# LayerNorm with a residual on one core: rows in DRAM blocks of 24, 24 and 16 per partition, and another list of 27 transfers

## The chip, the core and the metric

The kernel runs on one core of one Trainium2 chip. Its time is the device time of one execution in microseconds (us); the time of a version is the median over several runs. Before the change it is 237.93 us, from three runs between 237.87 and 237.95.

## What is computed

Two float32 tensors of 16 x 1024 x 512 are added, and each of the 16,384 rows of 512 numbers is normalised (mean, variance), scaled and shifted:

```python
def reference(x, residual, gamma, beta, eps):
    z = x + residual
    mean = np.mean(z, axis=-1, keepdims=True)
    var = np.var(z, axis=-1, keepdims=True)
    z_norm = (z - mean) / np.sqrt(var + eps)
    return (gamma * z_norm + beta).astype(np.float32)
```

x and residual are 33.55 MB each and so is the output: 100.66 MB have to be moved between DRAM and the core's memory (SBUF).

## The kernel before

The 16,384 rows are dealt to 128 partitions, so that each partition has 128 rows, and all counts below are rows per partition: one such row over all partitions is 128 x 512 numbers of 4 bytes, 262,144 bytes. The function `dram` (L73) says which rows of the DRAM tensor belong to which partition: the tensor is cut into blocks of `BLOCK` = 64 rows per partition, and within a block partition p has 64 rows that lie one behind the other in DRAM. A transfer must stay within one block (L65). A transfer of n rows takes from each partition one unbroken piece of n x 2 KiB; the pieces of two neighbouring partitions start 64 x 2 KiB = 128 KiB apart.

Two buffers in SBUF hold the data as rings: `zbuf` with 64 rows (x first, and later the results, in the same place), `rbuf` with 32 rows (residual first, then the sum). Row lo stands in slot lo modulo 64, or modulo 32.

`PLAN` (L19) is a list of words such as `x32+16`, load 16 rows of x from row 32 on; `r` is the residual, `o` a store of finished rows. SyncE (SP) issues the transfers strictly in this order at L140, all on one queue, and waits ahead of an issue where it has to:

- a load of x into slots that were used already waits until the stores of those rows have landed (L148, semaphores `so`),
- a load of residual into used slots waits until VectorE has read them (L154, `s_rstd` of the turn that read the last of them),
- a store waits until VectorE has finished its rows (L158, `s_out`).

While SP waits, all later issues of the list wait too. The first two issues (`EARLY`) are moved ahead of the barrier at the start of the program (L277).

The computation goes in turns of four rows, 32 turns:

- GpSimd (POOL) waits until the loads of both tensors that hold these rows have landed, and adds four rows in one instruction, rbuf = zbuf + rbuf (L178).
- ScalarE (ACT) waits for the sum and takes four row means with an accumulating activation (L201, a running sum of -z/512), four sums of squares (L211) and one square root for the four rows (L220). The activations' full results go to scratch (`junk_m`, `junk_s`).
- VectorE (DVE) waits for the square root, writes (sum - mean) x gamma into zbuf for four rows (L239), then the reciprocal of the root (L247), which also says that these rows of rbuf are free, and then multiplies by it and adds beta (L253), which says that the rows may be stored.

TensorE only spreads gamma and beta over the partitions at the start. ACT and DVE run loops, of 32 rows and of 64 rows per lap.

Of the kernel before, what the change touches and what calls it, by code (L numbers as in the profile page):

```python
# [8 lines left out]
FP32 = mybir.dt.float32  # L9
# [1 line left out]
ALU = mybir.AluOpType  # L11


BLOCK = 64
Z_ROWS = 64
R_ROWS = 32


PLAN = """  # L19
x0+8 r0+8 x8+8 r8+8 x16+16 r16+16 x32+16 r32+16 x48+16  # L20
o0+16 r48+16 x64+12 o16+20 r64+16 x76+24 r80+16 o36+28
r96+16 x100+8 x108+20 r112+4 r116+12
o64+16 o80+28 o108+12 o120+4 o124+4
"""


ADDS = [4] * 32


TURN = 4  # L30
R_TURNS = R_ROWS // TURN
Z_TURNS = Z_ROWS // TURN


EARLY = 2
# [3 lines left out]
def kernel(  # L39
# [9 lines left out]
    nc = tc.nc  # L49
    P = nc.NUM_PARTITIONS  # L50
# [3 lines left out]
    N, D = xf.shape  # L54
    inv_d = 1.0 / float(D)
    total = N // P


    tc.close()
    tc.compile()  # L60
# [1 line left out]
    moves = []  # L62
    for word in PLAN.split():
        kind, (lo, n) = word[0], map(int, word[1:].split("+"))
        assert lo // BLOCK == (lo + n - 1) // BLOCK  # L65
        moves.append((kind, lo, n))

    def of_kind(kind):
# [3 lines left out]

    def dram(t, lo, n):  # L73

        b0 = lo - lo % BLOCK
        v = t[P * b0 : P * (b0 + BLOCK), :].rearrange("(p j) d -> p j d", p=P)
        return v[:, lo - b0 : lo - b0 + n, :].rearrange("p a b -> p (a b)")

    zbuf = nc.alloc_sbuf_tensor("zbuf", [P, Z_ROWS * D], FP32)
# [4 lines left out]
    nm, ssq, std, rstd = (  # L84
        nc.alloc_sbuf_tensor(name, [P, R_ROWS], FP32) for name in ("nm", "ssq", "std", "rstd")
    )
    gamma_p = nc.alloc_psum_tensor("gamma_p", [P, D], FP32)
    beta_p = nc.alloc_psum_tensor("beta_p", [P, D], FP32)
    junk_m = [nc.alloc_psum_tensor(f"junk_m{i}", [P, D], FP32) for i in range(TURN)]
    junk_s = [nc.alloc_psum_tensor(f"junk_s{i}", [P, D], FP32) for i in range(6 - TURN)]  # L90
    junk_s += [
        nc.alloc_sbuf_tensor(f"junk_s{i}", [P, D], FP32) for i in range(6 - TURN, TURN)
    ]

    sems = []
# [1 line left out]
    def sem(name):  # L97
        s = nc.alloc_semaphore(name)
        sems.append(s)
        return s  # L100
# [5 lines left out]
    s_const = sem("const")  # L106
    s_pe = sem("pe")
    s_sum, s_mean, s_ssq, s_std = (
        [sem(f"{name}{j}") for j in range(R_TURNS)] for name in ("sum", "mean", "ssq", "std")
    )  # L110
    s_rstd = [sem(f"rstd{j}") for j in range(Z_TURNS)]
    s_out = sem("out")
    so = [sem(f"so{c}") for c in range(len(stores))]
    nums = [s.num for s in sems]
# [2 lines left out]
    def part(buf, size, lo, n):  # L117
        assert lo % size + n <= size
        return buf[:, (lo % size) * D : (lo % size + n) * D]
# [16 lines left out]
    seen = 0  # L136
    first = []

    def move(out, in_, s):
        i = nc.sync.dma_start(out=out, in_=in_).then_inc(s, 16)  # L140
        if len(first) < EARLY:
            first.append(i.ins)

    gone = 0
    for kind, lo, n in moves:
        if kind == "x":
            while gone < len(stores) and stores[gone][0] < lo + n - Z_ROWS:
                nc.sync.wait_ge(so[gone], 16)  # L148
                gone += 1
            move(part(zbuf, Z_ROWS, lo, n), dram(xf, lo, n), sx[loads_x.index((lo, n))])  # L150
        elif kind == "r":
            if lo + n > R_ROWS:
                last = (lo + n - R_ROWS) // TURN - 1
                nc.sync.wait_ge(s_rstd[last % Z_TURNS], last // Z_TURNS + 1)  # L154
            move(part(rbuf, R_ROWS, lo, n), dram(rf, lo, n), sr[loads_r.index((lo, n))])
        else:
            if lo + n > seen:
                nc.sync.wait_ge(s_out, lo + n)  # L158
                seen = lo + n
            move(dram(of, lo, n), part(zbuf, Z_ROWS, lo, n), so[stores.index((lo, n))])  # L160


# [5 lines left out]


    landed = {"x": 0, "r": 0}  # L170
    lo = 0
    for n in ADDS:
        for key, loads, s in (("x", loads_x, sx), ("r", loads_r, sr)):
            while landed[key] < len(loads) and loads[landed[key]][0] < lo + n:
                nc.gpsimd.wait_ge(s[landed[key]], 16)  # L175
                landed[key] += 1
        z = part(rbuf, R_ROWS, lo, n)
        nc.gpsimd.tensor_tensor(  # L178
            out=z, in0=part(zbuf, Z_ROWS, lo, n), in1=z, op=ALU.add
        ).then_inc(s_sum[lo // TURN % R_TURNS], 1)  # L180
        lo += n
    assert lo == total

# [1 line left out]
    def column(t, lo, n=1):  # L187
        return t[:, lo % R_ROWS : lo % R_ROWS + n]
# [5 lines left out]
    with act.Fori(0, total // R_ROWS) as lap:  # L194
        hints.append(act.mark_branch_hint_location())  # L195
        due = act.snap(lap + 1)
        for j in range(R_TURNS):
            rows = range(j * TURN, (j + 1) * TURN)
            act.wait_ge(s_sum[j], due)  # L199
            for k, r in enumerate(rows):  # L200
                i = act.activation(  # L201
                    out=junk_m[k][:, :],
                    in_=part(rbuf, R_ROWS, r, 1),
                    func=ACT.Identity,
                    scale=-inv_d,
                    accum_out=column(nm, r),
                )
            i.then_inc(s_mean[j], 1)
            act.wait_ge(s_mean[j], due)
            for k, r in enumerate(rows):  # L210
                i = act.activation(  # L211
                    out=junk_s[k][:, :],
                    in_=part(rbuf, R_ROWS, r, 1),
                    func=ACT.Square,
                    bias=column(nm, r),
                    accum_out=column(ssq, r),
                )
            i.then_inc(s_ssq[j], 1)
            act.wait_ge(s_ssq[j], due)
            act.activation(  # L220
                out=column(std, rows[0], TURN),
                in_=column(ssq, rows[0], TURN),
                func=ACT.Sqrt,
                bias=eps_t[:, 0:1],
                scale=inv_d,
            ).then_inc(s_std[j], 1)


    dve = nc.vector
    dve.wait_ge(s_pe, 2)  # L230
    with dve.Fori(0, total // Z_ROWS) as lap:  # L231
        hints.append(dve.mark_branch_hint_location())
        due = [dve.snap(lap * 2 + 1), dve.snap(lap * 2 + 2)]
        turn = dve.snap(lap + 1)
        for j in range(Z_TURNS):
            rows = range(j * TURN, (j + 1) * TURN)
            dve.wait_ge(s_std[j % R_TURNS], due[j // R_TURNS])
            for r in rows:
                dve.scalar_tensor_tensor(  # L239
                    out=part(zbuf, Z_ROWS, r, 1),  # L240
                    in0=part(rbuf, R_ROWS, r, 1),
                    scalar=column(nm, r),
                    in1=gamma_p[:, :],
                    op0=ALU.add,
                    op1=ALU.mult,
                )
            dve.reciprocal(  # L247
                out=column(rstd, rows[0], TURN), in_=column(std, rows[0], TURN)
            ).then_inc(s_rstd[j], 1)
            dve.wait_ge(s_rstd[j], turn)  # L250
            for r in rows:
                z = part(zbuf, Z_ROWS, r, 1)
                i = dve.scalar_tensor_tensor(  # L253
                    out=z,
                    in0=z,
                    scalar=column(rstd, r),
                    in1=beta_p[:, :],
                    op0=ALU.mult,
                    op1=ALU.add,
                )  # L260
            i.then_inc(s_out, TURN)


    loops = [b for b in nc.main_func.blocks if b.name.endswith("_loop")]
# [48 lines left out]
```

## Time and profile before

| | |
|---|---|
| median of the runs | 237.93 us |
| profiled execution, its own time | 237.87 us |
| its span, first to last instruction | 236.5 us |
| moved over DMA | 100.68 MB, mean 426 GB/s |
| ACT busy | 183.8 us, 78% |
| DVE busy | 177.2 us, 75% |
| POOL busy | 144.1 us, 61% |
| POOL waits for residual loads | 62.1 us, 9 times |
| ACT waits for POOL | 32.5 us, 6 times |
| SP waits for DVE's reciprocal (free slots of rbuf) | 126.9 us, 6 times |
| SP waits for finished rows (stores) | 54.8 us, 6 times |
| SP waits for landed stores (free slots of zbuf) | 33.6 us, 3 times |

How to read it: busy times are those of the engine's own instructions, within the span. SP's own waits are not busy time and cost nothing by themselves: the queue goes on with what SP issued earlier. The profiled execution has its own time; the 1.4 us between that and the span lie around the first and the last instruction.

The groups of instructions of one turn, with the count, the total busy time and the mean of one in ns, and behind the bar the idle time of the engine ahead of them:

```profile
L178 POOL TENSOR_TENSOR rbuf<-zbuf,rbuf 128x2048 f32<-128x2048 f32 x32 | 143.9, 4526 | 66.6 <-DMA rbuf<-in_residual_dram 62.1
L239 DVE SCALAR_TENSOR_TENSOR zbuf<-rbuf,nm,gamma_p 128x512 f32<-128x512 f32 x128 | 87.1, 743 | 46.5 <-ACT std L220 46.5
L201 ACT ACTIVATE junk_m<-rbuf 128x512 f32<-128x512 f32 x128 | 74.3, 580 | 32.7 <-POOL rbuf L178 32.5
L211 ACT ACTIVATE junk_s<-rbuf,nm 128x512 f32<-128x512 f32 x128 | 88.8, 694 | 1.0
```

And a part of the chain of waits (start in us, length in us, what), one turn from POOL to DVE and the next load that DVE releases:

```profile
119.84 4.53 POOL rbuf L178
...
141.73 2.46 ACT junk_m L201 x8
144.19 0.02 issue
144.21 2.94 ACT junk_s L211 x8
147.15 0.03 issue
147.17 0.30 ACT std L220
147.48 0.02 issue
147.50 2.72 DVE zbuf L239 x4
150.22 0.10 DVE rstd L247
150.32 0.02 issue
150.34 20.26 DMA rbuf<-in_residual_dram
```

POOL's adds begin at 12.23 us (the first two turns) and, for the third load of residual, at 41.44 us.

### The profile page before, as it was taken

The numbers are of one execution on the slowest core, as the hardware profiler recorded it, in microseconds if no ns is written. First come the engines' busy times: TensorE is split into PE (matmuls) and PEld (weight loads), VectorE is DVE, ScalarE is ACT, GpSimd is POOL, SyncE is SP. The second block draws the span as 40 slices with busy tenths as digits, with TensorE's granted clock in tenths as the row PEclk, the third lists the DMA queues.
The fourth block names the chain that finished last, engine by engine and source line by source line (L and its number), as shares of the span: only waits on it lengthen the run. The fifth ranks groups of instructions, "written<-read, shape, count | busy, mean of one in ns | idle before, by whom it ended". The sixth has DMA issues, their size and how long they took to land.

```text
span 236.5 us, 992 instructions
## 1 busy us (share of the span) xinstructions
PE 3.7 (2%) x4; PEld 1.2 (0%) x4; DVE 177.2 (75%) x290; ACT 183.8 (78%) x545; POOL 144.1 (61%) x36
## 2 busy tenths in 40 slices
PE   0600000000000000000000000000000000000000
PEld 0100000000000000000000000000000000000000
DVE  0001999629999999589990999889993999999930
ACT  2019997299999996899909999899939999999400
POOL 0098920999799306993079846993199498960000
DMA  8999999999999999998999999989999999998997
GB/s 316 438 435 435 421 438 443 443 443 443 427 371 438 443 421 423 470 436 384 443 449 474 391 427 499 398 389 432 416 454 429 417 442 435 489 436 388 411 410 327
DMA packets 3893, 100.68 MB, mean 426 GB/s; under 512 B 434, under 2 KB 434, under 8 KB 436
## 3 DMA queue, kind: packets, MB, share of 16 engines
q1 hardware_dynamic: 3888, 100.67, 99.4%
q14 instruction: 1, 0.01, 0.0%
q10 hardware_dynamic: 4, 0.00, 0.0%
HBM read 67.11 MB, written 33.55 MB: 426 GB/s over the span
## 4 chain that ended last, share of the span: by engine, by line
ACT 48%; DMA 35%; POOL 6%; DVE 4%; issue 1%; SPq 1%; ACTq 0%; DVEq 0%; POOLq 0%
DMA rbuf<-in_residual_dram 35%; ACT junk_s L211 25%; ACT junk_m L201 21%; POOL rbuf L178 6%; DVE zbuf L239 3%; ACT std L220 2%; DVE zbuf L253 1%; SPq L140 1%; DVE rstd L247 0%; ACTq L194 0%; DVEq L231 0%; ACTq L199 0%; POOLq L175 0%; ACTq L195 0%
## 5 line engine op out<-in xcount | busy, mean ns | idle before, releaser
L178 POOL TENSOR_TENSOR rbuf<-zbuf,rbuf 128x2048 f32<-128x2048 f32 x32 | 143.9, 4526 | 66.6 <-DMA rbuf<-in_residual_dram 62.1
L239 DVE SCALAR_TENSOR_TENSOR zbuf<-rbuf,nm,gamma_p 128x512 f32<-128x512 f32 x128 | 87.1, 743 | 46.5 <-ACT std L220 46.5
L201 ACT ACTIVATE junk_m<-rbuf 128x512 f32<-128x512 f32 x128 | 74.3, 580 | 32.7 <-POOL rbuf L178 32.5
L211 ACT ACTIVATE junk_s<-rbuf,nm 128x512 f32<-128x512 f32 x128 | 88.8, 694 | 1.0
L253 DVE SCALAR_TENSOR_TENSOR zbuf<-zbuf,rstd,beta_p 128x512 f32<-128x512 f32 x128 | 87.1, 743 | 1.1
L201 ACT ACTIVATION_READ_ACCUMULATOR junk_m<-rbuf 128x1 f32 x128 | 23.9, 187 | 0.0
L211 ACT ACTIVATION_READ_ACCUMULATOR junk_s<-rbuf,nm 128x1 f32 x128 | 23.9, 187 | 0.0
L220 ACT ACTIVATE std<-ssq,eps_t 128x4 f32<-128x4 f32 x32 | 9.5, 297 | 1.0
L247 DVE RECIPROCAL rstd<-std 128x4 f32<-128x4 f32 x32 | 5.4, 170 | 0.0
L192 ACT ACT_TABLE_LOAD x1 | 1.3, 1283 | 2.7 <-PEq L60 2.7
L131 PE MATMUL gamma_p<-gb_row,ones 1*128 1x512 f32 x2 | 2.0, 1118 | 7.0 <-DMA gb_row<-in_gamma_dram 7.0
L131 PE MATMUL beta_p<-gb_row,ones 1*128 1x512 f32 x2 | 1.9, 1052 | 0.0
L126 DVE MEMSET ones<- 1x128 f32 x1 | 0.2, 165 | 2.0 <-PEq L60 2.0
L131 PEld LDWEIGHTS beta_p<-gb_row,ones 1*128 1x128 f32 x2 | 0.7, 327 | 1.0 <-issue 0.5
L131 PEld LDWEIGHTS gamma_p<-gb_row,ones 1*128 1x128 f32 x2 | 0.5, 308 | 7.0 <-issue 7.0
L294 POOL MEMSET const-float32-0.0<- 128x1 f32 x1 | 0.1, 100 | 0.2 <-issue 0.2
L294 POOL MEMSET const-bfloat16-1.0<- 128x1 bf16 x1 | 0.1, 103 | 0.0
L294 POOL MEMSET const-uint8-127<- 128x1 uint8 x1 | 0.1, 103 | 0.0
L294 POOL MEMSET const-float32-1.0<- 128x1 f32 x1 | 0.1, 100 | 0.0
L127 DVE MEMSET eps_t<- 128x1 f32 x1 | 0.1, 59 | 0.0
## 6 DMA issues: line engine op xcount, KB each, us to landing
rbuf<-in_residual_dram SPq DMA_DIRECT2D x6, 4096.0 KB, 21.5
out_dram<-zbuf SPq DMA_DIRECT2D x2, 7168.0 KB, 31.5
zbuf<-in_x_dram SPq DMA_DIRECT2D x3, 4096.0 KB, 28.8
out_dram<-zbuf SPq DMA_DIRECT2D x2, 4096.0 KB, 33.9
zbuf<-in_x_dram SPq DMA_DIRECT2D x3, 2048.0 KB, 14.5
zbuf<-in_x_dram SPq DMA_DIRECT2D x1, 6144.0 KB, 24.0
out_dram<-zbuf SPq DMA_DIRECT2D x1, 5120.0 KB, 28.9
zbuf<-in_x_dram SPq DMA_DIRECT2D x1, 5120.0 KB, 26.3
```

The lines of the kernel that those rows point to most:

```text
L126: nc.vector.memset(ones[:, :], 1.0).then_inc(s_const, 1)
L131: nc.tensor.matmul(dest[:, :], ones[:, :], gb_row[:, k * D : (k + 1) * D], start=True, stop=True).then_inc(s_pe, 1)
L140: i = nc.sync.dma_start(out=out, in_=in_).then_inc(s, 16)
L178: nc.gpsimd.tensor_tensor(out=z, in0=part(zbuf, Z_ROWS, lo, n), in1=z, op=ALU.add).then_inc(s_sum[lo // TURN % R_TURNS], 1)
L192: act.preload_act_table_set("sqrt_and_others")
L201: i = act.activation(out=junk_m[k][:, :], in_=part(rbuf, R_ROWS, r, 1), func=ACT.Identity, scale=-inv_d, accum_out=column(nm, r),)
L211: i = act.activation(out=junk_s[k][:, :], in_=part(rbuf, R_ROWS, r, 1), func=ACT.Square, bias=column(nm, r), accum_out=column(ssq, r),)
L220: act.activation(out=column(std, rows[0], TURN), in_=column(ssq, rows[0], TURN), func=ACT.Sqrt, bias=eps_t[:, 0:1], scale=inv_d,).then_inc ...
L239: dve.scalar_tensor_tensor(out=part(zbuf, Z_ROWS, r, 1), in0=part(rbuf, R_ROWS, r, 1), scalar=column(nm, r), in1=gamma_p[:, :], op0=ALU.ad ...
L247: dve.reciprocal(out=column(rstd, rows[0], TURN), in_=column(std, rows[0], TURN)).then_inc(s_rstd[j], 1)
L253: i = dve.scalar_tensor_tensor(out=z, in0=z, scalar=column(rstd, r), in1=beta_p[:, :], op0=ALU.mult, op1=ALU.add,)
L294: nc = _bacc.Bacc("TRN2", target_bir_lowering=False, num_devices=1)
```

## The change

The rows are dealt to the partitions in blocks of 24, 24 and 16 rows, repeated (0 to 23, 24 to 47, 48 to 63, 64 to 87, 88 to 111, 112 to 127), in place of blocks of 64. The pieces of neighbouring partitions then start 48 KiB apart in blocks of 24 and 32 KiB apart in blocks of 16. A transfer of a whole block reads or writes one unbroken region of DRAM.

The list of transfers is another one; it has 27 words as before (6 of x, 12 of residual, 9 stores, where it had 9, 10 and 8). Every load of x is a whole block. The first load has 24 rows; the residual comes in loads of 8 and 16 rows. The rest of the diff makes the sizes of blocks and turns lists with a look-up (`edges`, `spot`), and with `TURNS = [4]` every turn has four rows, as before. The instructions of TensorE, VectorE, ScalarE and GpSimd are the same in number, form and order.

```diff
-BLOCK = 64
+BLOCKS = [24, 24, 16]

 PLAN = """
-x0+8 r0+8 x8+8 r8+8 x16+16 r16+16 x32+16 r32+16 x48+16
-o0+16 r48+16 x64+12 o16+20 r64+16 x76+24 r80+16 o36+28
-r96+16 x100+8 x108+20 r112+4 r116+12
-o64+16 o80+28 o108+12 o120+4 o124+4
+x0+24 r0+8 r8+16 x24+24 r24+8 x48+16 r32+16 o0+16 o16+8
+r48+16 x64+24 r64+16 o24+24 r80+8 r88+8 x88+24 r96+8 o48+16
+r104+8 r112+8 x112+16 r120+8 o64+24 o88+24 o112+8 o120+4 o124+4
 """
-ADDS = [4] * 32
-TURN = 4
+TURNS = [4]
...
+    def edges(sizes, end):
+        found, k = [0], 0
+        while found[-1] < end:
+            found.append(found[-1] + sizes[k % len(sizes)])
+            k += 1
+        assert found[-1] == end
+        return found
+
+    def spot(marks, row):
+        return max(k for k, m in enumerate(marks) if m <= row)
+
+    blocks = edges(BLOCKS, total)
+    marks = edges(TURNS, total)
...
     def dram(t, lo, n):
-        b0 = lo - lo % BLOCK
-        v = t[P * b0 : P * (b0 + BLOCK), :].rearrange("(p j) d -> p j d", p=P)
+        k = spot(blocks, lo)
+        b0, b1 = blocks[k], blocks[k + 1]
+        v = t[P * b0 : P * b1, :].rearrange("(p j) d -> p j d", p=P)
         return v[:, lo - b0 : lo - b0 + n, :].rearrange("p a b -> p (a b)")
...
             if lo + n > R_ROWS:
-                last = (lo + n - R_ROWS) // TURN - 1
-                nc.sync.wait_ge(s_rstd[last % Z_TURNS], last // Z_TURNS + 1)
+                last = spot(marks, lo + n - R_ROWS - 1)
+                nc.sync.wait_ge(s_rstd[last % z_turns], last // z_turns + 1)
...
             if lo + n > seen:
-                nc.sync.wait_ge(s_out, lo + n)
-                seen = lo + n
+                seen = next(m for m in marks if m >= lo + n)
+                nc.sync.wait_ge(s_out, seen)
```

More of the change, by code (lines that the diff above doesn't have):

```diff
@@ L19 @@
 PLAN = """
-x0+8 r0+8 x8+8 r8+8 x16+16 r16+16 x32+16 r32+16 x48+16
-o0+16 r48+16 x64+12 o16+20 r64+16 x76+24 r80+16 o36+28
-r96+16 x100+8 x108+20 r112+4 r116+12
-o64+16 o80+28 o108+12 o120+4 o124+4
-"""
-ADDS = [4] * 32
-TURN = 4
-R_TURNS = R_ROWS // TURN
-Z_TURNS = Z_ROWS // TURN
+x0+24 r0+8 r8+16 x24+24 r24+8 x48+16 r32+16 o0+16 o16+8
+r48+16 x64+24 r64+16 o24+24 r80+8 r88+8 x88+24 r96+8 o48+16
+r104+8 r112+8 x112+16 r120+8 o64+24 o88+24 o112+8 o120+4 o124+4
+"""
+TURNS = [4]
 EARLY = 2
@@ L56 @@
     total = N // P
+    def edges(sizes, end):
[9 more added lines that the diff above has]
+    marks = edges(TURNS, total)
+    most = max(TURNS)
+    r_turns, z_turns = spot(marks, R_ROWS), spot(marks, Z_ROWS)
+    assert marks[r_turns] == R_ROWS and marks[z_turns] == Z_ROWS
+    assert z_turns == 2 * r_turns
     tc.close()
@@ L64 @@
         kind, (lo, n) = word[0], map(int, word[1:].split("+"))
-        assert lo // BLOCK == (lo + n - 1) // BLOCK
+        assert spot(blocks, lo) == spot(blocks, lo + n - 1)
         moves.append((kind, lo, n))
@@ L88 @@
     beta_p = nc.alloc_psum_tensor("beta_p", [P, D], FP32)
-    junk_m = [nc.alloc_psum_tensor(f"junk_m{i}", [P, D], FP32) for i in range(TURN)]
-    junk_s = [nc.alloc_psum_tensor(f"junk_s{i}", [P, D], FP32) for i in range(6 - TURN)]
+    junk_m = [nc.alloc_psum_tensor(f"junk_m{i}", [P, D], FP32) for i in range(most)]
+    junk_s = [nc.alloc_psum_tensor(f"junk_s{i}", [P, D], FP32) for i in range(6 - most)]
     junk_s += [
-        nc.alloc_sbuf_tensor(f"junk_s{i}", [P, D], FP32) for i in range(6 - TURN, TURN)
+        nc.alloc_sbuf_tensor(f"junk_s{i}", [P, D], FP32) for i in range(6 - most, most)
     ]
@@ L108 @@
     s_sum, s_mean, s_ssq, s_std = (
-        [sem(f"{name}{j}") for j in range(R_TURNS)] for name in ("sum", "mean", "ssq", "std")
+        [sem(f"{name}{j}") for j in range(r_turns)] for name in ("sum", "mean", "ssq", "std")
     )
-    s_rstd = [sem(f"rstd{j}") for j in range(Z_TURNS)]
+    s_rstd = [sem(f"rstd{j}") for j in range(z_turns)]
     s_out = sem("out")
@@ L170 @@
     landed = {"x": 0, "r": 0}
-    lo = 0
-    for n in ADDS:
+    for k in range(len(marks) - 1):
+        lo, n = marks[k], marks[k + 1] - marks[k]
         for key, loads, s in (("x", loads_x, sx), ("r", loads_r, sr)):
@@ L179 @@
             out=z, in0=part(zbuf, Z_ROWS, lo, n), in1=z, op=ALU.add
-        ).then_inc(s_sum[lo // TURN % R_TURNS], 1)
-        lo += n
-    assert lo == total
+        ).then_inc(s_sum[k % r_turns], 1)
     def column(t, lo, n=1):
@@ L196 @@
         due = act.snap(lap + 1)
-        for j in range(R_TURNS):
-            rows = range(j * TURN, (j + 1) * TURN)
+        for j in range(r_turns):
+            rows = range(marks[j], marks[j + 1])
             act.wait_ge(s_sum[j], due)
@@ L220 @@
             act.activation(
-                out=column(std, rows[0], TURN),
-                in_=column(ssq, rows[0], TURN),
+                out=column(std, rows[0], len(rows)),
+                in_=column(ssq, rows[0], len(rows)),
                 func=ACT.Sqrt,
@@ L234 @@
         turn = dve.snap(lap + 1)
-        for j in range(Z_TURNS):
-            rows = range(j * TURN, (j + 1) * TURN)
-            dve.wait_ge(s_std[j % R_TURNS], due[j // R_TURNS])
+        for j in range(z_turns):
+            rows = range(marks[j], marks[j + 1])
+            dve.wait_ge(s_std[j % r_turns], due[j // r_turns])
             for r in rows:
@@ L247 @@
             dve.reciprocal(
-                out=column(rstd, rows[0], TURN), in_=column(std, rows[0], TURN)
+                out=column(rstd, rows[0], len(rows)), in_=column(std, rows[0], len(rows))
             ).then_inc(s_rstd[j], 1)
@@ L260 @@
                 )
-            i.then_inc(s_out, TURN)
+            i.then_inc(s_out, len(rows))
     loops = [b for b in nc.main_func.blocks if b.name.endswith("_loop")]
```

## The prediction

> **What bounds the kernel now.** I read the page's DMA rows first, then the stretches, then the SP issues in order of time, then the chain of waits. DMA rows of the page:
>
> ```profile
> DMA  8999999999999999998999999989999999998997
> DMA packets 3893, 100.68 MB, mean 426 GB/s; under 512 B 434, under 2 KB 434, under 8 KB 436
> q1 hardware_dynamic: 3888, 100.67, 99.4%
> ```
>
> The one queue that SP feeds is busy 99.4% of the span. 3888 is 27 transfers x 144: 128 data packets (one per partition) and 16 small ones each. The next view cuts the span into stretches; the last two columns are the DMA engines' busy share and GB/s.
>
> ```profile
> 0.00:6.00 6.00, 0.00 (x0) 0.00 (x0) 0.17 (x2) 1.28 (x1) 0.20 (x4) 1.00 0.86 320
> 6.00:18.00 12.00, 3.74 (x4) 1.15 (x4) 0.00 (x0) 1.25 (x5) 5.77 (x2) 1.00 1.01 430
> 18.00:60.00 42.00, 0.00 (x0) 0.00 (x0) 30.05 (x49) 35.46 (x107) 30.14 (x7) 1.00 1.01 434
> 60.00:80.00 20.00, 0.00 (x0) 0.00 (x0) 19.02 (x33) 19.58 (x59) 18.00 (x4) 1.00 1.01 423
> 80.00:120.00 40.00, 0.00 (x0) 0.00 (x0) 35.52 (x59) 35.02 (x105) 18.14 (x5) 1.00 1.01 434
> 120.00:160.00 40.00, 0.00 (x0) 0.00 (x0) 31.57 (x52) 34.11 (x102) 33.81 (x8) 1.00 1.00 433
> 160.00:200.00 40.00, 0.00 (x0) 0.00 (x0) 34.90 (x58) 36.06 (x109) 27.07 (x7) 1.00 1.00 429
> 200.00:230.00 30.00, 0.00 (x0) 0.00 (x0) 26.00 (x43) 21.02 (x64) 10.98 (x3) 1.00 1.00 433
> 230.00:236.50 6.50, 0.00 (x0) 0.00 (x0) 0.00 (x0) 0.00 (x0) 0.00 (x0) 1.00 0.77 324
> ```
>
> No long stretch exceeds 434 GB/s, whether it only loads (18 to 60) or mostly stores (200 to 230: 433). At 434 the 100.68 MB take 232.0 us; the span is 236.5, so 4.5 are lost, and each stretch's share is its length x (1 - GB/s / 434): start 1.58, 6 to 18 0.11, 60 to 80 0.51 (the first store falls there), 120 to 160 0.09, 160 to 200 0.46, 200 to 230 0.07, end 1.65. Sum 4.47. Start and end belong to any plan; 1.24 us in the middle is all that a plan could win.
>
> SP waits long, yet nothing starves, because it issues ahead:
>
> ```profile
> 42.70 0.33 SPq L140 DMA_DIRECT2D rbuf<-in_residual_dram  x1
> 71.94 0.33 SPq L140 DMA_DIRECT2D rbuf<-in_residual_dram  x1
> 80.99 0.33 SPq L140 DMA_DIRECT2D zbuf<-in_x_dram  x1
> 110.23 0.33 SPq L140 DMA_DIRECT2D zbuf<-in_x_dram  x1
> 226.90 0.33 SPq L140 DMA_DIRECT2D out_dram<-zbuf  x1
> ```
>
> I call "lead" the time from an issue until the queue has drained what stands ahead. One row of all partitions is 262,144 B, 0.604 us at 434 GB/s, so the transfers ahead have drained at 1.6 + 0.604 x their rows. For these five (r32+16, r48+16, x64+12, x76+24, o124+4: 80, 128, 144, 192, 380 rows ahead) that is 49.9, 78.9, 88.6, 117.6, 231.1, and the leads are 7.2, 7.0, 7.6, 7.4 and 4.2 us. So the chain of waits, which names ACT for 48%, doesn't set the end: it only has to keep the leads above nothing.
>
> **The change part by part.**
>
> *Transfers.* Still 27 (x 9 to 6, r 10 to 12, o 8 to 9), the same bytes, one packet per partition, hence again 3888 packets: 0 us. The 27 issues of 0.33 to 0.48 us lie inside leads. The first two issues still stand ahead of the start barrier and the last store is still 4 rows: start 1.58 and end 1.65 stay.
>
> *First load of 24 rows.* The first add needs x0+24 and r0+8, 32 rows where it was 16. Drained at 1.6 + 32 x 0.604 = 20.9; in before the same sum for 64 rows gives 40.3 and POOL started at 41.44, so 1.1 of landing: 22.0 against 12.23, 9.8 us later. What hides this is ACT's slack: it waits 32.5 us on POOL in before. Uncovered it would cost what exceeds the leads, so I follow the chain. POOL adds four rows in 4.5; ACT takes 5.75 per turn (2.46 + 2.94 + 0.30 and issue); DVE frees rbuf 2.85 after (2.72 + 0.10) and the rows are done 5.6 after. A load that waits for a store came 2.1 after the drain in before (o0+16: 78.9, x64+12 at 80.99).
>
> - r32+16 (waits for turn 3): 22.0 + 4.5 + 4 x 5.75 + 2.85 = 52.4; 96 rows ahead drain at 59.6; lead 7.2.
> - r48+16 (turn 7): 26.5 + 8 x 5.75 + 2.85 = 75.4; 136 rows, 83.7; lead 8.3.
> - x64+24 (waits for o16+8): 83.7 + 2.1 = 85.8; 152 rows, 93.4; lead 7.6.
> - r64+16 (turn 11; its first add needs r32+16, 112 rows): 69.2 + 1.1 + 4.5 + 4 x 5.75 + 2.85 = 100.7; 176 rows, 107.9; lead 7.2.
> - x88+24 (waits for o24+24, 216 rows): 132.1 + 2.1 = 134.2; 232 rows, 141.7; lead 7.5.
> - x112+16 (waits for o48+16, 280 rows): 170.7 + 2.1 = 172.8; 296 rows, 180.4; lead 7.6.
> - o88+24 (turn 27; turn 22 needs x88+24, 256 rows): 156.2 + 1.1 + 4.5 + 6 x 5.75 + 5.6 = 201.9; 344 rows, 209.4; lead 7.5.
> - o124+4: four turns later, 224.9; 380 rows, 231.1; lead 6.2.
>
> All others have more. The small residual loads in the second half add two waits on DVE (7 to 9); behind each stand the next issues of SP, x88, o48, r104 and so on, and all still come 7 us or more early. So every lead is as long as those with which before kept the queue at 1.00: 0 us. The nearest thing behind is turn 28: x112+16 lands at 191.1, its add ends at 195.6, ACT is free at 196.3; half a microsecond of slip there comes off leads of 6, not off the end.
>
> *Blocks.* Rows of one partition lie 48, 48 and 32 KiB apart per block instead of 128 KiB, and x loads of a whole block read one unbroken stretch of DRAM. No row of before shows another pitch, so I bound it. Best: everything lost in the middle goes, -1.24. Worst: the 33.55 MB of stores run at 423 instead of 434, the lowest long stretch: 79.3 - 77.3 = +2.0. I take 0, the nearest row being 434 for loads and 433 for stores, on either side the same figure, as if the queue's engines and not DRAM limited them.
>
> The Trainium skill ("DMA: Bandwidth & Descriptors", section on latency and other measured facts) reports that per-partition pitches of large powers of two cut a copy's rate (207 GB/s per direction at 512 KiB, 164 at 2 MiB, 103 at 4 MiB) and that a padded pitch restores it; it has no figure for 128 KiB, and 434 GB/s here leaves nothing to restore. By that rule the change could only win, by the rows nothing. "Perfetto Trace Analysis", section on DMA optimizations, speaks against the first part: smaller first pieces let work start sooner, where DMA engines are idle. By the rule the sum would be up to 237.87 + 9.8 = 247.7 with no lead; here the share is 1.01 from 6 us on, and the sum stays.
>
> *Sum.* 237.87 (profiled execution: span 236.5 and 1.4 around it; the median of the runs is 237.93) + 0 + 0 + 0 = 237.9.
>
> **The rivals.** (a) *The middle loss goes.* Block-wide loads avoid the 423 and 429 stretches: 0.51 + 0.46 and at most 1.24, so 236.6 to 237.4. For: 0.51 sits at one place, around the first store, and not at the later ones. Against: a first store comes in the new plan too, and five of the seven stretches between start and end are at 430 or above. (b) *DRAM addresses cost.* The 16-row blocks, a quarter of the bytes, keep a power of two as pitch, and stores of 24 rows write an unbroken 6 MiB. Price +2.0 if all stores run at 423: 239.9. It decides from 0.48 us on, that is from a mean of 433 instead of 434 over the span. Against: stores ran at 433. (c) *The queue runs empty.* The late first add is not caught up: 9.8 late less a lead of 6.2, 3.6 us: 241.5. It would need the chain 6 us longer than the sum above; against it stands that the last store comes out at 224.9, earlier than the 226.90 of before. (d) *The change does not do what it says*: excluded, since the list of the built program's instructions shows the new sizes and the new order on SP, and nothing else moved on any engine.
>
> **How the numbers follow.** No change (within 0.2%, 0.48 us, about what a measurement here can tell): 0.60. Faster, (a): 0.23. Slower: 0.17, of it (b) 0.13 and (c) 0.04. The time is that of the likeliest, 237.9. Its own range is 237.4 to 238.4; to hold 8 in 10 it reaches most of (a), 236.8, and more than half of (b), 239.2.
>
> **What would show it.** First add at 22 us; q1 with 3888 packets near 99.4%; long stretches at 434; the eight issues above within 2 us of the sum, the last store near 225 to 227. I am wrong if a stretch away from the ends falls below 420 with DMA share 1.00 (blocks), or if the DMA share falls (a lead used up), or if the loss of 60 to 80 us is gone.

## The result, and the profile after

The changed kernel takes 239.06 us (median of six runs, 238.80 to 240.17), before beside it 237.98 (six runs, 237.87 to 238.27): ratio 1.0052, 95% interval 1.0031 to 1.0073. It is slower by about half a per cent, where no change was forecast. The profiled execution of after took 239.55 us, half a microsecond more than its median, so the views below show somewhat more loss than most executions have.

The DMA rows of the page of after (busy tenths in 40 slices, GB/s in the same slices, the queue):

```profile
DMA  9989999999999999999999999999999999999895
GB/s 363 413 388 470 424 451 421 399 435 440 440 369 429 424 451 473 396 446 435 451 429 396 418 443 495 404 388 454 413 426 459 435 437 465 398 413 479 385 409 241
DMA packets 3893, 100.68 MB, mean 423 GB/s; under 512 B 434, under 2 KB 434, under 8 KB 436
q1 hardware_dynamic: 3888, 100.67, 98.8%
```

The packets are the same 3888. The share of the span is 98.8% where it was 99.4%, and what is missing stands in the last slice: 241 GB/s, where before has 327. The stretches of after, cut as in the prediction (last two columns: DMA share, GB/s):

```profile
0.00:6.00 6.00, 0.00 (x0) 0.00 (x0) 0.17 (x2) 1.28 (x1) 0.20 (x4) 1.00 0.98 361
6.00:18.00 12.00, 4.11 (x4) 0.99 (x4) 0.00 (x0) 0.00 (x0) 0.00 (x0) 1.00 0.93 402
18.00:60.00 42.00, 0.00 (x0) 0.00 (x0) 25.84 (x43) 32.25 (x96) 34.93 (x8) 1.00 1.01 436
60.00:80.00 20.00, 0.00 (x0) 0.00 (x0) 18.42 (x30) 16.14 (x50) 8.46 (x3) 1.00 0.99 409
80.00:120.00 40.00, 0.00 (x0) 0.00 (x0) 34.36 (x56) 38.33 (x116) 28.52 (x7) 1.00 1.01 436
120.00:160.00 40.00, 0.00 (x0) 0.00 (x0) 37.34 (x62) 38.33 (x115) 27.07 (x7) 1.00 1.00 430
160.00:200.00 40.00, 0.00 (x0) 0.00 (x0) 34.04 (x56) 35.29 (x107) 32.81 (x8) 1.00 1.01 434
200.00:230.00 30.00, 0.00 (x0) 0.00 (x0) 27.05 (x45) 22.06 (x66) 12.10 (x3) 1.00 0.99 429
230.00:238.20 8.20, 0.00 (x0) 0.00 (x0) 0.00 (x0) 0.00 (x0) 0.00 (x0) 1.00 0.68 286
```

The same reckoning, length x (1 - GB/s / 434): up to 60 us 1.70 (before 1.69), 60 to 230 us 1.68 (before 1.13), the end 2.80 (before 1.65). Together 6.18 against 4.47, and the spans are 238.2 and 236.5. A packet counts where it starts, so with larger pieces at the start the first two rows shift between each other; only their sum is to be read. Of the 1.7 us, 1.15 are at the end. The end in finer steps, first of before, then of after:

```profile
234.00:235.00 1.00, 0.00 (x0) 0.00 (x0) 0.00 (x0) 0.00 (x0) 0.00 (x0) 1.00 0.94 393
235.00:235.50 0.50, 0.00 (x0) 0.00 (x0) 0.00 (x0) 0.00 (x0) 0.00 (x0) 1.00 0.47 197
235.50:236.00 0.50, 0.00 (x0) 0.00 (x0) 0.00 (x0) 0.00 (x0) 0.00 (x0) 1.00 0.04 16
236.00:237.00 1.00, 0.00 (x0) 0.00 (x0) 0.00 (x0) 0.00 (x0) 0.00 (x0) 1.00 0.00 0
```

```profile
234.00:235.00 1.00, 0.00 (x0) 0.00 (x0) 0.00 (x0) 0.00 (x0) 0.00 (x0) 1.00 1.01 426
235.00:235.50 0.50, 0.00 (x0) 0.00 (x0) 0.00 (x0) 0.00 (x0) 0.00 (x0) 1.00 0.55 229
235.50:236.00 0.50, 0.00 (x0) 0.00 (x0) 0.00 (x0) 0.00 (x0) 0.00 (x0) 1.00 0.25 98
236.00:237.00 1.00, 0.00 (x0) 0.00 (x0) 0.00 (x0) 0.00 (x0) 0.00 (x0) 1.00 0.21 90
237.00:237.60 0.60, 0.00 (x0) 0.00 (x0) 0.00 (x0) 0.00 (x0) 0.00 (x0) 1.00 0.07 27
```

This is the view that names the loss. The share is a mean over 16 engines. Up to 235 us both kernels keep all of them busy. Then before falls from 0.47 to 0.04 within a microsecond, while after goes on for two microseconds with a quarter, a fifth and then a fifteenth of the engines: four, three, one. Most engines have finished; the program waits for a few that are behind.

The trace records start, length and size of each packet, not its engine. Since an engine starts a packet where its last one ended, the packets can be strung into 16 chains of 243 (27 transfers x 9). The table is worked out in this way; "spread" is the distance between the first and the last of the 16 chains when they finish a transfer.

```
kernel (profiled run)       spread behind the   spread behind the   at the end: mean,   profiled
                            first transfer      first store         last chain          time
before                      0.40                0.76                235.34, 236.01      237.87
after                       1.32                2.09                235.80, 237.70      239.55
E1 blocks of 64             0.57                0.76                235.62, 236.65      238.38
E2 first load 8 rows        1.20                1.74                235.84, 237.55      239.25
E4 first load 2 rows        0.49                0.58                235.45, 236.13      237.99
E9 only first 24 rows       1.04                1.30                235.82, 237.74      239.45
E15 one block of 128        0.76                0.85                236.10, 237.49      239.21
E16 the same, first 2 rows  0.52                0.63                236.21, 237.16      238.88
E18 first load 4 rows       0.41                0.62                235.52, 236.16      238.01
```

In every row the profiled time is the last chain's end plus 1.7 to 1.9 us. From before to after the mean end moves by 0.46 and the last chain by 1.69. The spread begins in the first packets: a packet of 48 KiB mostly takes 1.8 us, but the 16 first ones of after take between 1.9 and 3.7, four of them 2.86 or more. In E1 and E3 (described below), with the same 48 KiB at a pitch of 128 KiB, none takes over 2.8. The first ones of before (16 KiB, mostly 0.61) take 1.0 to 1.5. In after four chains are 0.59 to 0.86 us behind the mean of the 16 when they finish the first transfer, and no other is behind it at all; at the end again four stand out, 0.86 to 1.89 behind, the others at most 0.02.

The spread is never made up. That fits the stringing, in which each engine carries 9 of a transfer's 144 packets. It also grows: in after at the first store (1.34 to 2.09), and by about 0.6 at later places. In E9 most of it is growth: 1.04 at the start, 1.30 behind the first store, 2.07 behind r64+16 and 2.67 behind r96+8, both loads that stand right ahead of a store. So the first transfer starts the tail in after, and what comes later makes it longer. These are single profiled executions.

The Trainium skill ("DMA: Bandwidth & Descriptors", section on why a DMA increments its semaphore by 16 and not by 1) says that a transfer runs on up to 16 engines that finish independently and that only the full count means that all has landed. The trace agrees: POOL's first add, which needs all 16, starts at 22.87 us, 0.5 behind the last chain's 22.40 for r0+8, not behind the mean of 21.5.

SP's issues in after, for the prediction's list (start, length, what):

```profile
53.35 0.33 SPq L153 DMA_DIRECT2D rbuf<-in_residual_dram  x1
76.32 0.34 SPq L153 DMA_DIRECT2D rbuf<-in_residual_dram  x1
87.19 0.34 SPq L153 DMA_DIRECT2D zbuf<-in_x_dram  x1
103.08 0.33 SPq L153 DMA_DIRECT2D rbuf<-in_residual_dram  x1
135.71 0.33 SPq L153 DMA_DIRECT2D zbuf<-in_x_dram  x1
174.55 0.33 SPq L153 DMA_DIRECT2D zbuf<-in_x_dram  x1
227.95 0.33 SPq L153 DMA_DIRECT2D out_dram<-zbuf  x1
```

The eighth of the list, o88+24, was issued at 204.98. They come 0.9 to 3.1 us behind the sum (52.4, 75.4, 85.8, 100.7, 134.2, 172.8, 201.9, 224.9), three of them by more than 2 us (r64+16, o88+24, o124+4), and the shortest lead by the sum's own drain times is 231.1 - 227.95 = 3.2 us. The queue never ran empty.

### The profile page after: what moved, and what is told of

It is laid out like the page before. It is cut to its first block, busy times and chain, and to the rows that moved or that the text cites. A ratio compares the mean times of both kernels' runs of the same rounds, so it can differ in the third digit from the quotient of the medians.

```text
span 238.2 us, 993 instructions
## 1 busy us (share of the span) xinstructions
PE 4.1 (2%) x4; PEld 1.0 (0%) x4; DVE 177.2 (74%) x290; ACT 183.7 (77%) x545; POOL 144.1 (60%) x36
## 3 DMA queue, kind: packets, MB, share of 16 engines
q1 hardware_dynamic: 3888, 100.67, 98.8%
## 4 chain that ended last, share of the span: by engine, by line
ACT 43%; DMA 40%; POOL 6%; DVE 6%; issue 1%; SPq 0%; ACTq 0%; DVEq 0%; POOLq 0%
ACT junk_s L222 22%; ACT junk_m L212 19%; DMA rbuf<-in_residual_dram 17%; DMA out_dram<-zbuf 13%; DMA zbuf<-in_x_dram 10%; POOL rbuf L191 6%; DVE zbuf L250 3%; ACT std L231 2%; DVE zbuf L264 2%; SPq L153 0%; DVE rstd L258 0%; ACTq L205 0%; DVEq L242 0%; ACTq L210 0%; ACTq L206 0%
```

## The experiments

Each ran against the kernel before on the same chip; times are medians, ratios are to before with a 95% interval. E1 to E4 ran together, then E5 to E8, E9 to E11, E12, E13 to E15, and E16 to E18.

**E1, the new list with the old blocks.**

```diff
-BLOCKS = [24, 24, 16]
+BLOCKS = [64]
```

> The new list of transfers with the old blocks of 64 rows; nothing is left out. Theory S (the queue engines get out of step on the first, 48 KiB pieces, and the end waits for the one furthest behind): as slow as the changed kernel, about 239.1, with a tail after 235 us in which the DMA share is below 0.6. Theory L (the 48 and 32 KiB pitch in DRAM costs): back to 238.0. Theory C (the chain comes late because the first add does): about 239.1, but with a DMA share under 1 in the middle.

238.28 us, ratio 1.0009 (0.9998 to 1.0020). The layout undone takes back about 0.8 of the 1.1 us. Theory L has the place right; S and C as stated fall, since the first load of 24 rows and its late add are still there.

**E2, the first loads cut, the new blocks kept.**

```diff
-x0+24 r0+8 r8+16 x24+24
+x0+8 r0+8 x8+16 r8+16 x24+24
```

> The changed kernel with its first loads cut to x 8, residual 8, x 16, residual 8 to 24; blocks of 24, 24 and 16 stay; nothing is left out. Theory S: 238.0 (first pieces of 16 KiB as before). Theory L: 239.1. Theory C: about 238.0 with the first add near 12 us.

239.01 us, ratio 1.0036 (1.0021 to 1.0051): still slow with first pieces of 16 KiB, except in two of its nine executions (238.03 and 238.16), so the size of before's first pieces does not repair it reliably, and a region read without a break is not needed for it.

**E3, the list and blocks of before with a first load of 24 rows.**

```diff
-x0+8 r0+8 x8+8 r8+8 x16+16 r16+16 x32+16 r32+16 x48+16
+x0+24 r0+8 r8+8 x24+8 r16+16 x32+16 x48+16 r32+16
```

> The list and the blocks of before, but the first load has 24 rows (and the loads around it are cut to suit, x48+16 going ahead of r32+16); nothing is left out. Theory S: 239.0. Theory L: 238.0. Theory C: 239.0 with a DMA share under 1 somewhere in the middle.

237.98 us, ratio 1.0001 (0.9992 to 1.0010). A first add 10 us later costs nothing, and neither do first pieces of 48 KiB when the pitch is 128 KiB.

**E4, the changed kernel with a first load of 2 rows.**

```diff
-x0+24 r0+8 r8+16
+x0+2 r0+8 x2+22 r8+16
```

> The changed kernel with its first load cut into 2 rows and 22 rows, the first residual load of 8 rows between them; one transfer more; nothing is left out. Theory S: the first packets are 4 KiB, so 238.0 or a little less, although the first add still comes near 22 us. Theory L: 239.1. Theory C: 239.1.

238.02 us, ratio 1.0003 (0.9994 to 1.0011): the whole loss is gone, with the blocks of 24, 24 and 16 everywhere and the late first add. Its end, in the steps used above:

```profile
234.00:235.00 1.00, 0.00 (x0) 0.00 (x0) 0.00 (x0) 0.00 (x0) 0.00 (x0) 1.00 0.95 401
235.00:235.50 0.50, 0.00 (x0) 0.00 (x0) 0.00 (x0) 0.00 (x0) 0.00 (x0) 1.00 0.62 262
235.50:236.00 0.50, 0.00 (x0) 0.00 (x0) 0.00 (x0) 0.00 (x0) 0.00 (x0) 1.00 0.08 33
236.00:237.00 1.00, 0.00 (x0) 0.00 (x0) 0.00 (x0) 0.00 (x0) 0.00 (x0) 1.00 0.00 0
```

The engines finish together again. E1 and E4 undo quite different things, the pitch and the size of the very first packets, and each takes the long tail away. So the theory became P: the pitch matters while the engines start on the first transfer.

**E5, only the first 64 rows in the old block.**

```diff
-BLOCKS = [24, 24, 16]
+BLOCKS = [64, 24, 24, 16]
```

> The list of the changed kernel; the first 64 rows in one block as before (128 KiB pitch), the second 64 in blocks of 24, 24 and 16. Theory P (the pitch matters only while the queue's engines start on the first transfer; E1 and E4 point to it): as E1, 238.3 (238.0 to 238.5). Theory L (the pitch costs throughout): half way, 238.65 or more.

238.31 us, ratio 1.0010 (1.0001 to 1.0018), as E1: the blocks of the second half cost nothing more than a block of 64 there.

**E9, only the first 24 rows in the new block.**

```diff
-BLOCKS = [24, 24, 16]
+BLOCKS = [24, 40, 64]
```

> The list of the changed kernel; blocks of 24, 40 and 64 rows: only the first 24 rows keep the 48 KiB pitch, the next 40 have 80 KiB, the second half 128 KiB. Theory P (the pitch matters only while the queue's engines start on the first transfer): as the changed kernel, 239.0, the tail after 235.5 us as long. If it is the sum of many blocks: 238.5 or less.

239.32 us, ratio 1.0049 (1.0036 to 1.0062): all of the loss is there, with only the first 24 rows at 48 KiB. The test is not quite clean, since rows 24 to 63 have 80 KiB, the pitch of neither kernel, and by the table most of the profiled execution's spread came after the first transfer. Its end is the long one again:

```profile
235.00:235.50 0.50, 0.00 (x0) 0.00 (x0) 0.00 (x0) 0.00 (x0) 0.00 (x0) 1.00 0.62 262
235.50:236.00 0.50, 0.00 (x0) 0.00 (x0) 0.00 (x0) 0.00 (x0) 0.00 (x0) 1.00 0.44 180
236.00:237.00 1.00, 0.00 (x0) 0.00 (x0) 0.00 (x0) 0.00 (x0) 0.00 (x0) 1.00 0.08 33
237.00:237.60 0.60, 0.00 (x0) 0.00 (x0) 0.00 (x0) 0.00 (x0) 0.00 (x0) 1.00 0.06 27
```

**E18, a first load of 4 rows.**

```diff
-x0+24 r0+8 r8+16
+x0+4 r0+8 x4+20 r8+16
```

> E4 with a first load of 4 and 20 rows in place of 2 and 22, blocks of 24, 24 and 16. If only the very first packet of an engine is late: between E2 (first load of 8 rows, 239.0) and E4 (2 rows, 238.0), about 238.4.

238.12 us, ratio 1.0000 (0.9992 to 1.0009). Four rows cure it as well as two; the step between that was expected did not come. With E2 the bound lies between 4 and 8 rows.

**Which pitch? E6, E7, E10, E13, E14, E15.** Two readings were tried: that a pitch has to be a power of two, and that the 16 engines' first addresses must not lie close together. E6 and E7 use the list of before (E6 with o16+20 cut in two), the others the new list.

```diff
+BLOCKS = [32, 32, 64]   # E6, 64 KiB
+BLOCKS = [16, 48, 64]   # E7, 32 KiB
+BLOCKS = [48, 16, 64]   # E10, 96 KiB
+BLOCKS = [88, 24, 16]   # E13, 176 KiB
+BLOCKS = [112, 16]      # E14, 224 KiB
+BLOCKS = [128]          # E15, 256 KiB
```

> The list of before (o16+20 cut into 16 and 4 rows) with blocks of 32, 32 and 64: pitch 64 KiB at the start, 8-row first loads. Theory P with the reach of addresses as cause (the closer together the 16 engines' first addresses, the wider they start): 238.3 to 238.8. Theory P with powers of two as the good pitch: 238.0.

> The list of before with blocks of 16, 48 and 64: pitch 32 KiB at the start, 8-row first loads. Theory P with the reach of addresses as cause: 239.0 or more, the worst of all. Theory P with powers of two as the good pitch: 238.0.

> The list of the changed kernel; blocks of 48, 16 and 64 rows, so that the first load has a pitch of 96 KiB and is no unbroken region. Theory P with any pitch that is no power of two as cause: 238.8 to 239.1. Theory P with the close or unbroken region as cause: 238.3 as with blocks of 64.

> The list of the changed kernel, blocks of 88, 24 and 16: first pitch 176 KiB, no power of two. If pitches that are no power of two make the spread: 238.8 to 239.3. If closeness of the first addresses makes it: 238.3 as with 64.

> The list of the changed kernel, blocks of 112 and 16: first pitch 224 KiB, no power of two. If pitches that are no power of two make the spread: 238.8 to 239.3. If closeness makes it: 238.3.

> The list of the changed kernel, one block of 128: pitch 256 KiB, a power of two. Either reading: 238.3, as with 64. If it is slower than that, large pitches cost by themselves.

- 64 KiB: 238.36, ratio 1.0008 (1.0000 to 1.0017).
- 32 KiB: 238.07, ratio 1.0019 (1.0005 to 1.0033); of twelve executions four took 238.87 to 239.37, the others 237.84 to 238.33.
- 96 KiB: 238.86, ratio 1.0027 (1.0012 to 1.0043); four took 237.75 to 238.15, eight 238.76 to 239.68.
- 176 KiB: 238.92, ratio 1.0042 (1.0030 to 1.0054).
- 224 KiB: 238.84, ratio 1.0036 (1.0025 to 1.0048); two of eight took 238.10 and 238.21.
- 256 KiB: 238.98, ratio 1.0035 (1.0022 to 1.0048).

Neither reading holds. Closeness falls with 176 and 224 KiB, a power of two with 256. With 32, 96 and 224 KiB, and in E2 with 48, one and the same program does well in some executions and badly in others, as an accident of how the engines fall into step would; that it is one is not shown. Only 64 KiB was good throughout (238.06 to 238.45). With 128 KiB most executions were below 238.7, but not all: two of E17's twelve took 239.54 and 240.32, one of E12's eleven 238.88, and of the 146 executions of before in all sessions one took 239.22. What of a pitch does it stays open.

**E16, E17, small first loads with other blocks.** E15 and E1 with the first load cut as in E4.

```diff
 BLOCKS = [128]           # E16; [64] in E17
-x0+24 r0+8 r8+16
+x0+2 r0+8 x2+22 r8+16
```

> E15 (one block of 128) with the first load cut into 2 and 22 rows as in E4. If the spread at the start is the seed here too: 238.0 to 238.3. If a 256 KiB pitch costs at the switches from loads to stores by itself: 238.8 to 239.0.

> E1 (the new list with blocks of 64) with the first load cut into 2 and 22 rows. If what is left of the list's own cost is also the start: 238.0. If it is the list's later part: 238.3.

E16: 239.15, ratio 1.0050 (1.0037 to 1.0064). The cure of E4 does not work at 256 KiB. The chains are 0.52 apart behind the first transfer and still 0.63 apart behind the first store; then the spread grows to 1.00 at r64+16, and to 1.83 at r120+8, both loads ahead of a store. The mean of the 16 chains ends late too, at 236.21 against 235.45 in E4. So that layout has a cost of its own, at the switches from loads to stores, which is not that of the changed kernel. E17: 238.37, ratio 1.0026 (1.0009 to 1.0042), the median as E1: the 0.3 us that the new list costs with blocks of 64 do not come from the first packets. Nor are they the list's alone, since E4 has the same list with the blocks of 24, 24 and 16 and does not pay them. Where they come from wasn't found.

**E8, the first store one place earlier, and E11, the output touched before.** Both kernels lose time ahead of the first store, 0.64 us per engine in before and about 0.8 in after.

```diff
-x32+16 r32+16 x48+16 o0+16
+x32+16 r32+16 o0+16 x48+16
```

> The kernel before with its first store moved one place up, ahead of x48+16 (96 rows ahead of it in place of 112); nothing is left out. The stretch of lower rate that before and after both have near 67 to 71 us: if the first store makes it, it moves to 57 to 61 us; if it belongs to a time or to ScalarE's lap, it stays at 67 to 71. Time 238.0 either way.

238.18 us, ratio 1.0005 (0.9996 to 1.0014). The low stretch moves with the store. Before, then E8:

```profile
50.00:62.00 12.00, 0.00 (x0) 0.00 (x0) 9.88 (x17) 11.87 (x36) 10.51 (x4) 1.00 1.02 437
62.00:74.00 12.00, 0.00 (x0) 0.00 (x0) 11.57 (x20) 11.67 (x37) 12.00 (x3) 1.00 1.01 412
```

```profile
50.00:62.00 12.00, 0.00 (x0) 0.00 (x0) 9.83 (x17) 11.87 (x37) 9.76 (x4) 1.00 1.00 399
62.00:74.00 12.00, 0.00 (x0) 0.00 (x0) 11.58 (x20) 11.67 (x36) 12.00 (x3) 1.00 1.01 437
```

412 and 399 GB/s stand in the stretch that holds the last loads ahead of the first store, and the other stretch is at 437: the first store makes it, not a time.

```diff
+        if at == EARLY:
+            nc.sync.dma_start(out=of[0:16, :], in_=xf[0:16, :]).then_inc(s_touch, 16)
+        if (kind, lo, n) == ("o",) + stores[0]:
+            nc.sync.wait_ge(s_touch, 16)
```

> The kernel before with one transfer more: third in the list, 16 rows of x are copied to the output's first rows (they are overwritten by the first store, which waits for the copy). If the slow stretch ahead of the first store is the first touch of the output tensor, it is gone at 67 to 71 us, part of it hides behind the start, and the time falls by 0.2 to 0.6, to 237.4 to 237.8. If it belongs to the first store from SBUF itself, it stays and the time is 238.0 to 238.3.

238.11 us, ratio 1.0004 (0.9996 to 1.0013). The packets of x48+16 still take 0.67 us more per engine than packets of their size mostly do (0.64 in before). A first write to the output, of 16 rows of 2 KiB and so 32 KiB in all, doesn't take it away; a larger one was not tried.

**E12, the kernel before with a first load of 2 rows.**

```diff
-x0+8 r0+8 x8+8
+x0+2 r0+8 x2+6 x8+8
```

> The kernel before with its first load cut into 2 rows and 6 rows; one transfer more; nothing is left out. If small first packets help whatever the pitch, the start costs less and the time is 237.6 to 237.8, faster than both kernels. If they only repair the spread that the 48 KiB pitch makes, 237.95 to 238.1, no change.

237.95 us, ratio 1.0006 (0.9996 to 1.0016). Small first packets repair a start that is out of step; where it is in step they give nothing. No version tried beats the kernel before.

## Why the prediction was wrong

*What bounds the kernel.* Right: the DMA queue, with all engines busy until the last microseconds, and no lead was used up. The wins that were bounded at 1.24 us did not come.

*Transfers.* Right on the packets, 3888 again. Wrong in the sentence "start 1.58 and end 1.65 stay". This is the step of the sum that failed, together with the 0 for the blocks below: the end was taken as a matter of the last store alone, still 4 rows. It measured 2.80 in place of 1.65, and that is where most of what the blocks cost came out. The end is also the place where any spread of the 16 engines is paid, and the formula for the drain, 1.6 + 0.604 x rows, treats them as one pipe and cannot see it.

*First load of 24 rows.* Right: POOL started at 22.87 against 22.0 reckoned, and E3 shows by itself that the late first add is free. POOL's row in after:

```profile
22.87 8.95 POOL L191 TENSOR_TENSOR rbuf<-zbuf,rbuf 128x2048 f32<-128x2048 f32 x2 [22.43 <-DMA rbuf<-in_residual_dram]
```

The issues came up to 3.1 us later than the sum, where 2 was allowed. In E4, whose engines stay together, the same eight came 0.1 to 1.7 us behind it, so the spread accounts for 0.8 to 1.5 of it: each add waits for the engine furthest behind. The rest stands in E4 too and has another reason.

*Blocks.* Taken as 0, with -1.24 and +2.0 as bounds. The place was right: E1, E5 and E9 put the cost in the blocks, and of these in the first one. The size was 0.8 us by E1 (239.06 against 238.28, from different sessions) and 1.0 by E4 (238.02), within the bounds, but those were worked out for other mechanisms. The reason given for the 0 was too narrow: a stretch's mean rate of 434 says nothing about packets that start at once from rest, and the first row of the table of stretches, 320 GB/s, was booked under "Start and end belong to any plan".

*The rivals.* (b) had the right sign and the right object, DRAM addresses, and the wrong mechanism: stores did not run slower for long. From 200 to 230 us they ran at 429 against 433, which is 0.28 us. That the upper end of the range, 239.2, stretched towards its price of 239.9, covers 239.06 is luck. (c) did not happen. (a) did not happen: the slow stretch at the first store stayed, and E8 shows that it belongs to that store.

*The signs.* A stretch did fall below 420 away from the ends: 409 at a share of 0.99 from 60 to 80 us. It is not the sign of the blocks' loss that it was meant to be. E18, with the same blocks and no loss, has 412 there, and E1, with blocks of 64, 405.

*What is shown and what is not.* Shown: the blocks' loss needs the new pitch in the first 24 rows (E1, E5, E9) and a large first load (E4, E18, E2), and with it goes the tail of a few late engines. Shown as well: a spread that is there stays. Not shown: why 48 KiB puts the engines out of step, what makes the spread grow at loads ahead of stores, and the 0.3 us of the list with blocks of 64.

The skill's rule on row pitch ("DMA: Bandwidth & Descriptors", latency and other measured facts: large powers of two lose rate, a padded pitch restores it) does not describe this case; its figures begin at 512 KiB. A pitch of 48 KiB, no power of two, was slower than 128 KiB, and the cost at 256 KiB was 0.35% (0.22 to 0.48), in E16 at the loads ahead of stores and not from a lower rate throughout.

## What to carry to other kernels

When the DMA queue is busy from end to end, look at its last microseconds in half-microsecond steps: a share that fell slowly, from 0.55 to 0.07 in two microseconds, meant here that single engines were behind, and a mean rate over a long stretch hides that. Such a lag can be made by the first transfer, and here no later part of the list repaired it; a first transfer of a few rows is a cheap way to test for it. Change one block or one piece of a layout at a time: here the first load of 24 of 128 rows decided over the loss.

## What the runs showed of the hardware that had not been expected

- The 16 engines of a queue keep the distance they start with: 1.32 us behind the first transfer of after was 1.34 behind x48+16, 44 us and 72 rows later. It grows where stores follow loads.
- The first packets of an execution take much longer than others of their size: 1.0 to 1.5 us in place of 0.61 for 16 KiB at 128 KiB pitch, up to 3.7 in place of 1.8 for 48 KiB at 48 KiB pitch, and up to 2.8 for 48 KiB at 128 KiB pitch (E1, E3).
- The first store slows the last load packet ahead of it on every engine, and on some the one before that too: 0.64 us in all per engine in before and about 0.8 in after. It moves with the store (E8); the load ahead of the next store that follows loads, o24+24 in after, is r64+16, and it loses about 0.05.
